# The second stream of a two-layer encoder: its loads on another queue, its multiplies behind another instruction, a third buffer

## The chip, the cores and the metric

The kernel runs on one core of one Trainium2 chip. The metric is the device time of one execution in microseconds (us); lower is better. TensorE is called PE, VectorE DVE, ScalarE ACT, GpSimd POOL and SyncE SP. A "q" behind an engine's name (SPq, ACTq) is its sequencer, which issues transfers and waits for semaphores.

## The reference, cut to what matters

Two layers over 256 positions of width 2048, batch 1, float32. Before each layer, six modulation vectors of 2048 are computed from one conditioning vector `c` by a matrix of 2048 x 12288 a layer; they shift, scale and gate the two halves of the layer.

```python
c_act = jax.nn.silu(c)
for l in range(DEPTH):                                   # DEPTH = 2
    mod = c_act @ ada_w[l] + ada_b[l]                    # [1, 6 * 2048]
    sh1, sc1, g1, sh2, sc2, g2 = split(mod, 6)
    h = rmsnorm(x, norm_mix_g[l]) * (1.0 + sc1) + sh1
    y = four_mixers(h @ w_in[l] + b_in[l])               # rglru, attention, hyena, mlstm
    x = x + g1 * (y @ w_out[l])
    h = rmsnorm(x, norm_ffn_g[l]) * (1.0 + sc2) + sh2
    x = x + g2 * ((silu(h @ w1[l]) * (h @ w3[l])) @ w2[l])
return rmsnorm(x, final_g)
```

## The kernel before, in words

Activations lie transposed (features on the 128 partitions, 256 positions on the free axis). All weights of the large products are streamed once from HBM in tiles of 128 x 1024 float32 (512 KB, called `raw`; 764 in all), in one order written out in `weight_items`.

**The weight stream.** A tile passes through four engines. SP loads it into one of six `raw` buffers (L327). ACT rounds it to `hi` (L342), DVE computes the remainder `lo = raw - hi` (L343), and PE multiplies with both (L389, L391 to L393), which gives nearly float32 precision. `hi` and `lo` have three buffers each, so a rounding waits until PE is done with the tile three places earlier. `fetch` keeps loads six tiles and the splits three tiles ahead of PE in program order; the splits have a raised priority. The first eight k-blocks of layer 0's input projection are used unsplit (L386).

**The modulation stream.** The matrix of the modulation, transposed, is 192 blocks of 128 output columns, each in two halves of 128 x 1024: 384 half columns of 512 KB. They do not go through PE. For each one `ada_load` loads a half column (tile `ada`, or `ad` from another pool for some of the first 64), and `ada` multiplies it on DVE by the broadcast activation `cb` and sums along the row (L465, with a short second instruction that reads the sum). The first 64 run ahead of layer 0; the other 320 are spread by `RATES` over the weight tiles: after the products of each tile, `ada(rate)` adds the rate to an account, and each whole unit emits one multiply. The rate is 1 a tile in layer 0's mixer and output projection, about 0.53 (8/15, then 28/53) in layer 0's feed-forward part, 24/43 in layer 1's mixer, and small after that; the last multiply comes early in layer 1's feed-forward part.

**The order.** Each engine runs its instructions strictly in order. The order is made at build time by a list scheduler with a simulated clock: an instruction is taken when its inputs are ready by that clock, earlier ones in program order first. `issue_after(ins)` adds one bound: what the block emits stands behind `ins` if it is on the same engine. So the loads of the modulation (`load`, L315) stand on SP's queue behind the latest weight load `self.last`; the multiplies stand behind one early instruction of the first norm (`self.after`) and are otherwise free. From the 59th multiply on, `ada_load` keeps two half columns loaded or under way, the one about to be multiplied included, in two buffers (`NADA` = 2).

**Transfers.** All transfers of the kernel share eight completion semaphores in turn, so that a transfer also waits until the one eight places before it has landed.

Of the kernel before, what the change touches and what calls it, by code (L numbers as in the profile page):

```python
# [11 lines left out]
F32 = mybir.dt.float32  # L12
F32R = mybir.dt.float32r
AF = mybir.ActivationFunctionType
ALU = mybir.AluOpType
# [218 lines left out]
class Lazy:  # L234


    def __init__(self, n, make):
        self.n, self.make, self.made = n, make, []
# [8 lines left out]


class Net:
    NRAW, NHL, NADA = 6, 3, 2  # L250

    BUFS = dict(h=16, y=16, p=4, s=10, e=9)
    TAGS = dict(h="h", w3="y", pl="s",
# [5 lines left out]
    def __init__(self, ctx, tc, d):  # L259
        self.tc, self.nc, self.d = tc, tc.nc, d  # L260
        self.n = 0
        self.last = self.after = None
        e = ctx.enter_context
        self.cp = e(tc.tile_pool(name="cp", bufs=1))
        self.wp = e(tc.tile_pool(name="wp", bufs=self.NHL))
        self.sp = e(tc.tile_pool(name="sp", bufs=1))
        self.tp = e(tc.tile_pool(name="tp", bufs=5))
        self.yp = e(tc.tile_pool(name="yp", bufs=12))
        self.pa = e(tc.tile_pool(name="pa", bufs=3, space=PSUM))
        self.pm = e(tc.tile_pool(name="pm", bufs=5, space=PSUM))  # L270
        nc = self.nc
        self.par = self.cp.tile([P, DEPTH, NPAR], F32, name="par")
        nc.sync.dma_start(self.par, d["par"])
        self.ident = self.cp.tile([P, P], F32, name="ident")
        nc.sync.dma_start(self.ident, d["k_ident"])
        self.misc = self.cp.tile([P, 16], F32, name="misc")
        nc.sync.dma_start(self.misc, d["k_misc"])
        self.one = self.misc[:, 0:1]
# [52 lines left out]
    def _split(self):  # L331
        k = self.n_split
        n, whole = self.items[k][1:]
        t = self.raw.pop(k)
        self.n_split += 1
        if whole:
            self.hl[k] = (t, None)
            return
        with self.tc.high_priority(offset=1500):
            hi = self.wp.tile([P, 1024], F32R, tag="hi", name=self.nm("hi"))  # L340
            lo = self.wp.tile([P, 1024], F32R, tag="lo", name=self.nm("lo"))
            self.nc.scalar.activation(hi[:, :n], t[:, :n], AF.Copy)  # L342
            self.nc.vector.tensor_tensor(lo[:, :n], t[:, :n], hi[:, :n].bitcast(F32), ALU.subtract)  # L343
        self.hl[k] = (hi, lo)

    def fetch(self):
# [91 lines left out]

    def ada_load(self):

        at = self.ada_at
        while self.ada_got < min(len(self.ada_items), at + (6 if at < 58 else self.NADA)):
            n = self.ada_got
            l, b, h = self.ada_items[n]
            if n < 64 and n % 3:
                t = self.pair("ad")
            else:
                t = self.wp.tile([P, 1024], F32, tag="ada", name=self.nm("ada"), bufs=self.NADA)
            self.load(t, self.d["ada"][l, b, :, h * 1024:(h + 1) * 1024])
            self.ada_tiles[n] = t  # L450
            self.ada_got += 1

    def ada(self, n):

        nc = self.nc
        self.ada_left += n
        while self.ada_left >= 0.999 and self.ada_at < len(self.ada_items):
            self.ada_left -= 1
            self.ada_load()
            l, b, h = self.ada_items[self.ada_at]  # L460
            t = self.ada_tiles.pop(self.ada_at)
            self.ada_at += 1
            acc, mod = self.acc[l], self.mod[l]
            with self.tc.issue_after(self.after) if self.after else nullcontext():
                nc.vector.scalar_tensor_tensor(t, t, 1.0, self.cb[:, h * 1024:(h + 1) * 1024], ALU.mult, ALU.mult,  # L465
                                               accum_out=acc[:, b, h:h + 1])
            j, k = b // 16, b % 16
            if h == 0:
                continue
            if l == 0 and j < 2:  # L470
                m = mod[:, b:b + 1]
                nc.vector.scalar_tensor_tensor(m, acc[:, b, 0:1], acc[:, b, 1:2], self.pc(l, "ada_b", b), ALU.add, ALU.add)
                if j:
                    nc.vector.scalar_tensor_tensor(self.gain[l, j][:, k:k + 1], m, 1.0, self.pc(l, "nmix", k), ALU.add, ALU.mult)
            elif k == 15:
                c = slice(j * 16, j * 16 + 16)
                nc.vector.tensor_tensor(mod[:, c], acc[:, c, 0], acc[:, c, 1], ALU.add)
                nc.vector.tensor_tensor(mod[:, c], mod[:, c], self.pc(l, "ada_b", j * 16, 16), ALU.add)
                if j in (1, 4):
                    nc.vector.scalar_tensor_tensor(self.gain[l, j], mod[:, c], 1.0, self.pc(l, "nmix" if j == 1 else "nffn", 0, 16),  # L480
                                                   ALU.add, ALU.mult)
# [775 lines left out]
```

## Time and profile before

| | |
|---|---|
| time, median of 3 runs | 2627.47 us (2624.53 to 2630.35) |
| the profiled execution: its time, its span | 2628.5 us, 2626.7 us |
| PE, DVE, ACT busy share of the span | 95%, 70%, 44% |
| mean granted TensorE clock | 0.981 of full speed |
| moved by DMA | 629.63 MB, mean 240 GB/s |
| roundings, remainders | 737 each, mean 1038 and 1210 ns |
| multiplies of the modulation | 384, mean about 1250 ns |

Read it as follows. The busy share of PE counts matmuls whose ends are modelled; where PE waits for a weight tile, this shows as idle time of its weight load (PEld) and of the matmul behind it. A wait is put down to what ended it. Idle time of the other three engines costs nothing unless PE waits for it later. By the norms' instructions in the trace, the time falls into five stages: up to 204 us the start (filters, first 64 half columns), to 621 us layer 0's mixer and output projection, to 1411 us its feed-forward part, to 1865 us layer 1's mixer and output projection, to 2616 us its feed-forward part.

### The profile page before, as it was taken

Reading aid. Unit: us, or ns where it says so; the run is one execution under the profiler, and the core shown is the slowest. Engines: PE = TensorE matmul, PEld = TensorE weight load, DVE = VectorE, ACT = ScalarE, POOL = GpSimd, SP = SyncE. Lnnn points to the kernel's source line nnn. Section 1 sums busy time; section 2 is a strip of 40 time slices with the busy share of each in tenths; the row PEclk is TensorE's granted clock in tenths of the full one; section 3 lists DMA queues with packets and bytes.
Section 4 is the critical chain, followed back from the end, with each engine's and each line's share of the span. In section 5 each row is a group of like instructions: output and inputs, shape, how many; then the busy total and the mean of one; then the engine's idle time right before and its main releaser. Section 6 shows DMA issues by size and latency. Waiting matters only on the chain. (4 is left out here: it accounts for less than half of the span.)

```text
span 2626.7 us, 38926 instructions
## 1 busy us (share of the span) xinstructions
PE 2503.5 (95%) x14962; PEld 2167.8 (83%) x14962; DVE 1827.2 (70%) x2862; ACT 1164.0 (44%) x1790; POOL 157.3 (6%) x142
## 2 busy tenths in 40 slices
PE   7989989998999999999998998999899999999998
PEld 3468878798888888778888998989888888888887
DVE  6987576688777677776788767776765555555555
ACT  4432343444444344334444445554444444434443
POOL 2101010020000000000011110002100000000001
PEclk9889999999999999999999999999899999999999
DMA  7988777688888888788887766657666665665564
GB/s 260 351 312 270 242 258 243 206 290 283 275 273 297 264 266 278 264 266 270 266 283 249 267 230 224 218 178 246 221 218 188 187 191 187 185 190 191 188 182 132
DMA packets 180719, 629.63 MB, mean 240 GB/s; under 512 B 20162, under 2 KB 20371, under 8 KB 180531
## 3 DMA queue, kind: packets, MB, share of 16 engines
q1 hardware_dynamic: 177076, 620.84, 71.5%
q10 hardware_dynamic: 3456, 6.29, 0.6%
q8 instruction: 117, 1.92, 0.3%
q14 instruction: 70, 0.57, 0.1%
HBM read 618.67 MB, written 8.39 MB: 239 GB/s over the span
## 5 line engine op out<-in xcount | busy, mean ns | idle before, releaser
L342 ACT ACTIVATE hi<-raw 128x1024 fp32r<-128x1024 f32 (+2 forms) x737 | 763.7, 1038 | 801.7 <-PE a L389 340.4
L393 PE MATMUL a<-h,lo 128*128 128x256 f32 x3848 | 1077.4, 286 | 25.8 <-DVE lo L343 25.2
L343 DVE TENSOR_TENSOR lo<-raw,hi 128x1024 fp32r<-128x1024 f32 (+2 forms) x737 | 887.5, 1210 | 281.5 <-ACT hi L342 280.8
L389 PE MATMUL a<-h,hi 128*128 128x512 f32 x2624 | 914.8, 397 | 0.0
L393 PEld LDWEIGHTS a<-h,lo 128*128 128x128 f32 x3848 | 733.4, 192 | 57.8 <-DVE lo L343 45.3
L465 DVE SCALAR_TENSOR_TENSOR ada<-ada,cb 128x1024 f32<-128x1024 f32 x342 | 425.8, 1246 | 392.8 <-DMA ada<-in_ada 392.3
L389 PEld LDWEIGHTS a<-h,hi 128*128 128x128 f32 x2624 | 485.5, 188 | 108.2
L389 PE MATMUL a<-g,hi 128*128 128x512 f32 x1352 | 463.0, 396 | 0.0
L393 PE MATMUL a<-g,lo 128*128 128x256 f32 x1408 | 370.8, 280 | 5.6 <-DVE lo L343 5.3
L391 PE MATMUL a<-h,hi 128*128 128x256 f32 x1224 | 363.0, 299 | 10.5 <-ACT h L549 6.7
L392 PE MATMUL a<-h,hi 128*128 128x256 f32 x1224 | 359.0, 294 | 6.1 <-DVE h L551 6.1
L393 PEld LDWEIGHTS a<-g,lo 128*128 128x128 f32 x1408 | 264.0, 188 | 23.7 <-DVE lo L343 12.2
L389 PEld LDWEIGHTS a<-g,hi 128*128 128x128 f32 x1352 | 243.3, 188 | 47.9
L391 PEld LDWEIGHTS a<-h,hi 128*128 128x128 f32 x1224 | 240.8, 198 | 18.2 <-ACT h L549 8.0
L392 PEld LDWEIGHTS a<-h,hi 128*128 128x128 f32 x1224 | 241.5, 197 | 12.4 <-DVE h L551 7.1
L514 POOL TENSOR_TENSOR sq<-sq,sq 128x256 f32<-128x256 f32 x65 | 71.6, 1102 | 1717.0 <-issue 1405.4
L386 PE MATMUL a<-h,raw 128*128 128x256 f32 x688 | 167.5, 395 | 3.3 <-DMA raw<-in_w_in 3.3
L386 PEld LDWEIGHTS a<-h,raw 128*128 128x128 f32 x688 | 132.7, 198 | 34.6 <-issue 12.5
L1151 DVE SCALAR_TENSOR_TENSOR x<-a,mod,x 128x256 f32<-128x256 f32 x228 | 100.3, 476 | 22.6 <-PE a L393 22.6
L1172 ACT ACTIVATE s<-s 128x256 f32<-128x256 f32 x82 | 34.3, 418 | 115.2 <-DVE s L1169 115.2
L1168 ACT ACTIVATE s<-a 128x256 f32<-128x256 f32 x82 | 31.5, 384 | 114.0 <-PE a L393 114.0
L415 ACT ACTIVATE g<-s 128x256 fp32r<-128x256 f32 x88 | 36.1, 410 | 68.2 <-DVE s L1173 62.9
(268 smaller groups left out, 2188.5 us busy)
## 6 DMA issues: line engine op xcount, KB each, us to landing
raw<-in_w SPq DMA_DIRECT2D x496, 512.0 KB, 4.7
ada<-in_ada SPq DMA_DIRECT2D x342, 512.0 KB, 6.1
raw<-in_w_in SPq DMA_DIRECT2D x168, 512.0 KB, 5.5
raw<-in_w_out SPq DMA_DIRECT2D x64, 512.0 KB, 5.7
ad<-in_ada SPq DMA_DIRECT2D x42, 512.0 KB, 7.9
raw<-in_w SPq DMA_DIRECT2D x32, 384.0 KB, 3.2
spectra<-sl ACTq DMA_DIRECT2D x24, 256.0 KB, 6.9
spec<-spectra SPq DMA_DIRECT2D x24, 256.0 KB, 6.3
```

The costliest lines, as they stand in the source:

```text
L342: self.nc.scalar.activation(hi[:, :n], t[:, :n], AF.Copy)
L343: self.nc.vector.tensor_tensor(lo[:, :n], t[:, :n], hi[:, :n].bitcast(F32), ALU.subtract)
L386: mm(o, hi[:, c], a[:, :T], start=first and b == 0, stop=last, skip_group_check=True)
L389: mm(ps[b], hi[:, c], a, start=first, stop=False, skip_group_check=True)
L391: mm(o, hi[:, c], a[:, :T], start=first and b == 0, stop=False, skip_group_check=True)
L392: mm(o, hi[:, c], a[:, T:], start=False, stop=False, skip_group_check=True)
L393: mm(o, lo[:, c], a[:, :T], start=False, stop=last, skip_group_check=True)
L415: self.nc.scalar.activation(dst[:, :T], src, AF.Copy)
L465: nc.vector.scalar_tensor_tensor(t, t, 1.0, self.cb[:, h * 1024:(h + 1) * 1024], ALU.mult, ALU.mult, accum_out=acc[:, b, h:h + 1])
L514: nc.gpsimd.tensor_tensor(self.sq, self.sq, t, ALU.add)
L1151: i = self.nc.vector.scalar_tensor_tensor(self.x[k], o, g, self.x[k], ALU.mult, ALU.add)
L1172: nc.scalar.activation(s, s, AF.Silu)
```

## The change

From the 65th half column on (`n >= 64`) the load is issued by ACT instead of SP, and stands behind the latest rounding emitted so far (`self.hi_at`), not behind the latest weight load. Each multiply also stands behind the latest remainder emitted so far (`self.lo_at`). The `ada` tile has three buffers instead of two, and two half columns are kept loaded or under way as before. The rates, the number of transfers and their sizes stay.

```diff
 class Net:
-    NRAW, NHL, NADA = 6, 3, 2
+    NRAW, NHL, NADA = 6, 3, 3
...
         self.last = self.after = None
+        self.hi_at = self.lo_at = None
...
-            self.nc.scalar.activation(hi[:, :n], t[:, :n], AF.Copy)
-            self.nc.vector.tensor_tensor(lo[:, :n], t[:, :n], hi[:, :n].bitcast(F32), ALU.subtract)
+            self.hi_at = self.nc.scalar.activation(hi[:, :n], t[:, :n], AF.Copy).ins
+            self.lo_at = self.nc.vector.tensor_tensor(lo[:, :n], t[:, :n], hi[:, :n].bitcast(F32), ALU.subtract).ins
...
     def ada_load(self):
+        nc = self.nc
         at = self.ada_at
-        while self.ada_got < min(len(self.ada_items), at + (6 if at < 58 else self.NADA)):
+        while self.ada_got < min(len(self.ada_items), at + (6 if at < 58 else self.NADA - 1)):
...
-            self.load(t, self.d["ada"][l, b, :, h * 1024:(h + 1) * 1024])
+            src = self.d["ada"][l, b, :, h * 1024:(h + 1) * 1024]
+            if n >= 64:
+                with self.tc.issue_after(self.hi_at) if self.hi_at else nullcontext():
+                    nc.scalar.dma_start(t, src)
+            else:
+                self.load(t, src)
...
-            with self.tc.issue_after(self.after) if self.after else nullcontext():
+            with (self.tc.issue_after(self.after) if self.after else nullcontext()), \
+                    (self.tc.issue_after(self.lo_at) if self.lo_at else nullcontext()):
                 nc.vector.scalar_tensor_tensor(t, t, 1.0, self.cb[:, h * 1024:(h + 1) * 1024], ALU.mult, ALU.mult,
                                                accum_out=acc[:, b, h:h + 1])
```

## Rows read from the trace of the kernel before

**Rows 1.** Windows, one for each stage: busy us by engine, granted clock, DMA share, GB/s.
```profile
204.00:621.00 417.00, 390.10 (x2466) 348.69 (x2464) 294.56 (x514) 162.35 (x296) 45.90 (x42) 0.98 0.76 256
621.00:1411.00 790.00, 763.56 (x4360) 653.58 (x4360) 587.89 (x866) 345.36 (x475) 14.31 (x14) 0.99 0.82 272
1411.00:1865.00 454.00, 433.50 (x3198) 406.75 (x3198) 331.87 (x543) 230.81 (x382) 49.94 (x43) 0.97 0.68 227
1865.00:2616.00 751.00, 745.40 (x4360) 654.82 (x4360) 444.77 (x590) 342.14 (x472) 12.41 (x14) 0.99 0.60 186
```
**Rows 2.** Waits of PEld, stages two to five: us in total, times, longest us.
```profile
PEld a L393 <- DVE lo L343: 5.8, 6, 2.0
...
PEld a L393 <- DVE lo L343: 45.7, 63, 3.3
...
PEld a L393 <- DVE lo L343: 7.5, 6, 3.8
...
PEld a L393 <- DVE lo L343: 0.5, 1, 0.5
```
**Rows 3.** Waits of DVE for the modulation's loads, stages two, three and four.
```profile
DVE ada L465 <- DMA ada<-in_ada: 100.3, 65, 3.8
...
DVE ada L465 <- DMA ada<-in_ada: 189.2, 105, 4.4
...
DVE ada L465 <- DMA ada<-in_ada: 89.7, 46, 6.0
```
**Rows 4.** DVE, timeline around one such wait in stage three.
```profile
913.58 1.22 DVE L343 TENSOR_TENSOR lo<-raw,hi 128x1024 fp32r<-128x1024 f32 x1
919.04 1.23 DVE L465 SCALAR_TENSOR_TENSOR ada<-ada,cb 128x1024 f32<-128x1024 f32 x1 [4.23 <-DMA ada<-in_ada]
...
920.52 1.22 DVE L343 TENSOR_TENSOR lo<-raw,hi 128x1024 fp32r<-128x1024 f32 x1
```
**Rows 5.** PE, the same timeline.
```profile
920.05 0.63 PE L389 MATMUL a<-h,hi 128*128 128x512 f32 x2
921.79 0.51 PE L393 MATMUL a<-h,lo 128*128 128x256 f32 x2 [1.11 <-DVE lo L343]
```
**Rows 6.** SP's queue, the same timeline.
```profile
909.13 1.85 SPq L327 DMA_DIRECT2D raw<-in_w  x2
911.03 0.42 SPq L315 DMA_DIRECT2D ada<-in_ada  x1
```
**Rows 7.** The tile ada: multiplies of stages two, three, four; landing in stage three.
```profile
L465 DVE SCALAR_TENSOR_TENSOR ada<-ada,cb x97: 1210/1225/2295, 204.1 to 619.7; 128x1024 f32<-128x1024 f32 x97
...
L465 DVE SCALAR_TENSOR_TENSOR ada<-ada,cb x144: 1208/1225/1384, 623.9 to 1393.7; 128x1024 f32<-128x1024 f32 x144
DMA to landing us min/median/max: 4.2/6.3/8.4
...
L465 DVE SCALAR_TENSOR_TENSOR ada<-ada,cb x65: 1210/1225/1753, 1413.4 to 1847.9; 128x1024 f32<-128x1024 f32 x65
```
**Rows 8.** ACT, timeline in stage five, after the last multiply.
```profile
2120.74 1.06 ACT L342 ACTIVATE hi<-raw 128x1024 fp32r<-128x1024 f32 x1 [1.93 <-PE a L389]
2123.56 1.06 ACT L342 ACTIVATE hi<-raw 128x1024 fp32r<-128x1024 f32 x1 [1.76 <-PE a L389]
```
**Rows 9.** DVE, the same stretch.
```profile
2121.84 1.23 DVE L343 TENSOR_TENSOR lo<-raw,hi 128x1024 fp32r<-128x1024 f32 x1 [2.03 <-ACT hi L342]
2124.65 1.22 DVE L343 TENSOR_TENSOR lo<-raw,hi 128x1024 fp32r<-128x1024 f32 x1 [1.59 <-ACT hi L342]
```
**Rows 10.** The tile spectra: ACT's only transfers, all in the first stage.
```profile
L684 ACTq DMA_DIRECT2D spectra<-sl x24: 326/334/975, 80.1 to 161.7; - x24
...
DMA to landing us min/median/max: 5.3/6.7/8.7
```
**Rows 11.** Waits of ACT in stage two.
```profile
ACT L846 <- DVE v L842: 18.4, 1, 18.4
```
**Rows 12.** Windows of 65.7 us: the slice with the highest DMA rate.
```profile
65.70:131.40 65.70, 59.58 (x170) 31.46 (x168) 59.37 (x123) 29.21 (x58) 11.80 (x6) 0.90 0.93 351
```

## The prediction, made before the changed kernel was run

> **What bounds the kernel now.** I read the windows by stage first. Stages three and five are the feed-forward parts of the two layers and do the same work on PE: 4360 matmuls each. Stage three takes 790 us and stage five 751 us, a difference of 39 us [rows 1]. What differs is the modulation: 144 multiplies lie in stage three [rows 7], and stage five holds only its last few. So 39 us is about what the second stream costs layer 0's feed-forward part, and it is the largest thing that a change to this stream alone can win there. In stage five PE is busy 745 of 751 us, so the tensor work itself is the floor.
>
> Next, the waits of PE's weight loads, stage by stage. In stage three they wait 63 times, 45.7 us in all, for a remainder from DVE; in stage five 0.5 us in all; in the two mixers 5.8 and 7.5 us [rows 2]. DVE is busy only 588 of 790 us in stage three [rows 1], so it is late and not overloaded. The waits of DVE say why: 105 of the 144 multiplies wait for their load, 189 us in all, 1.8 us each on average [rows 3].
>
> The timeline shows one case from cause to effect. SP issues two weight loads and, behind them, a load of the modulation at 911.03 [rows 6]. DVE finishes a remainder at 914.80, then comes to the multiply, whose half column is there only at 919.04, 8.0 us after its issue: 4.23 us idle. The next remainder starts at 920.52 [rows 4], and PE, out of split tiles, idles 1.11 us before the matmul that needs it [rows 5]. The roundings and remainders hold only three tiles, so DVE standing still for that long empties them.
>
> The landing in stage three takes 4.2 to 8.4 us, median 6.3 [rows 7]. As the mean wait is 1.8 us over the stalled ones, the built order puts a multiply some 4.5 to 5 us behind the issue of its load, earlier than the load can be there. That, not the rate of the transfers, is the fault: stage three moves 272 GB/s [rows 1], and the first part of the kernel reached 351 [rows 12].
>
> **The change, part by part.** *The distance from load to multiply.* After the change a load stands behind the latest rounding, and its multiply, emitted one unit of the account later, behind the remainder that is the latest by then. In stage three a unit comes every 1.9 tiles, so two tiles lie between in about 8 of 9 cases and one in the others. I take the tile's rhythm from stage five, where nothing disturbs it: roundings start 2.82 us apart (2120.74, 2123.56) and last 1.06 [rows 8]; a remainder starts 1.10 behind its rounding and lasts 1.23 [rows 9]. The load goes out 1.06 us after the start of its rounding. With two tiles between, the multiply can start at 2 x 2.82 + 1.10 + 1.23 = 7.97 on the same scale, 6.9 us behind the issue; with one tile, 4.1 us. Against the median landing of 6.3 that is no wait in most two-tile cases (I estimate 0.3 us on average from the spread up to 8.4), and about 2.2 us in the one-tile cases. Sum over 144: 128 x 0.3 + 16 x 2.2 = 74 us of DVE waiting in place of 189.
>
> *What that is worth on PE.* A remainder ends 2.33 us after its buffer comes free and is needed two tiles later, at 5.64: 3.3 us to spare. A multiply takes 1.2 of them [rows 7], so about 2 us of waiting is still hidden. Only the one-tile cases reach past that, by some tenths; with the activations' work that DVE also does between, I leave 6 us of the 39. Bounds: nothing gained here (the landing moves with the issue), and 39 us gained. I take 33, near the upper end, because the stalls of [rows 3] are the one difference between stages three and five.
>
> *The load's issue on ACT.* ACT's only transfers now took 334 ns each to issue, at most 975, and the sequencer does nothing else meanwhile [rows 10]. 320 loads make 107 us. In stage three that is 144 x 0.33 = 48 us more on an engine busy 345 of 790 [rows 1], just behind a rounding, with the next rounding free to start only when PE gives up a buffer: ACT sat idle 1.76 us for that [rows 8]. Hidden there. In the mixers, 97 + 65 loads [rows 7] make 54 us on an engine busy 162 of 417 and 231 of 454 us; a chain that runs through ACT (softmax, gates) can meet some of it. Between 0 and 54 us; I take 2 us, near zero, because of the idle time. If a load had to wait for its buffer on ACT, every rounding behind it would wait too. The third buffer excludes this: the load that is emitted just before multiply m needs the buffer of multiply m - 2, a unit or more old.
>
> *SP's queue.* It loses 320 loads, and weight loads no longer stand behind one. In stages three and five roundings wait for PE and not for weights, so nothing is won there. Some waits for a weight tile in the mixers may go; I count nothing.
>
> *The mixers.* DVE's waits for loads there, 100 and 90 us [rows 3], shrink in the same way, less in stage two, where a unit comes every tile and the distance is 4.1 us. PE's waits for remainders there are 5.8 + 7.5 = 13.3 us [rows 2], the most that can be won by this way; I take 4 us. The first 64 half columns keep their queue; the third buffer for a third of them I count at nothing, for lack of any wait of PE on them in these rows.
>
> The Trainium skill, "DMA: Bandwidth & Descriptors", section "Issuing engines are not separate DMA queues", says that transfers issued from different engines run on the same 16 DMA engines and that a second issuing engine saves only the sequencer's issue time. The trace can't test this for these loads, as all stand on SP's queue. By that rule alone the landing stays at its 6.3 us, which is what the sum above uses; the sum holds only through the distance, and if the rule were wrong and loads landed near their fastest 4.2 us, even one-tile cases would be nearly free and the gain would be 39 + 4.
>
> **The sum.** 33 (stage three) + 4 (mixers) - 2 (issue on ACT) = 35 us. The profiled execution took 2628.5 us, 1.0 above the median; 2628.5 - 35 = 2593.5, and against the median 2592.5. I say **2593 us**.
>
> **Rivals.**
> *The multiply still comes too early.* If the schedule's clock lets the load go out on ACT later than behind its rounding (ACT's queue is in order, and in stage two it stood 18.4 us for one DVE result [rows 11]), or lets only one tile lie between, the waits stay near 2 us and move rather than go. For it: the order is built with a clock that took landing for 4.5 to 5 us. Against it: the two new bounds hold in any order. A load that is late by one tile in all of stage three returns to 4.1 us of distance and 2.2 us of waiting, more than the 1.8 of now: the 33 us are lost, and with the mixers' small sums the time is 2622 to 2633. This is also where the skill's rule leads if the distance did not grow. Chance 0.12.
>
> *Half of it.* The distance grows, but DVE, with the multiplies now bunched behind remainders, misses the spare 3.3 us more often. Half of the 33 is kept: 2606 to 2622. Chance 0.10.
>
> *Slower: the issue delays what stands behind it on ACT in the mixers.* There a rounding shares ACT with the softmax, the gates and the evacuation of PSUM, and PE waits on results of these chains. If each of the 162 loads put its 334 ns into such a chain, that costs 54 us; with 33 won in stage three the time is 2628.5 - 33 + 54 = 2649. The point from which it decides: more than 38 us, so 0.24 us for each of the 162, or an issue that takes up to the 975 ns of [rows 10] and holds roundings in stage three as well. Against it: ACT is idle half of the mixers, and only one instruction in many there is one that PE waits for. Chance 0.13, 2634 to 2665.
>
> **How the numbers follow.** The forecast, 2580 to 2606, has 0.65. Its own range comes from the bounds: 39 + 13 gained at the most (2577), 20 at the least. Half 0.10, nothing 0.12, slower 0.13. For 8 in 10 the range takes the forecast, the half and a part of the nothing: 2581 to 2627. A measurement of this kernel tells 0.2%, 5 us, from no change: faster (below 2622) is the forecast and the half, 0.75; same 0.11; slower 0.14.
>
> **What the changed profile would show.** Right: stage three 755 to 762 us for the same 4360 matmuls; PE's weight loads waiting for remainders there under 10 us instead of 45.7; DVE's waits for the modulation's loads there below 80 us; issues of `ada` on ACT's queue of about 0.33 us, each right behind a rounding; the landing unchanged at about 6 us or shorter. Stages two and four within 5 us of 417 and 454. Wrong: stage three above 775 us, with DVE still waiting at the multiplies; or ACT's roundings waiting for the issue of a load, or for its buffer, and with them a longer stage two or four.

## The result and the profile after

The changed kernel took 2562.75 us (median of 4 runs, 2561.3 to 2564.05) against 2626.09 us for the kernel before on the same chip (median of 4 runs, 2624.53 to 2630.35). The ratio is 0.9756, 95% interval 0.9739 to 0.9773: 2.4% faster, and faster than the range that was forecast (2581 to 2627).

The page of the changed kernel, parts 1 and 3: busy time, and the transfers by queue. Below it are the same rows of the kernel before.

```profile
PE 2470.3 (96%) x14962; PEld 2164.6 (85%) x14962; DVE 1839.4 (72%) x2862; ACT 1160.4 (45%) x1788; POOL 151.6 (6%) x142
...
q1 hardware_dynamic: 130996, 453.05, 53.9%
q10 hardware_dynamic: 49536, 174.09, 19.3%
```
```profile
PE 2503.5 (95%) x14962; PEld 2167.8 (83%) x14962; DVE 1827.2 (70%) x2862; ACT 1164.0 (44%) x1790; POOL 157.3 (6%) x142
...
q1 hardware_dynamic: 177076, 620.84, 71.5%
q10 hardware_dynamic: 3456, 6.29, 0.6%
```

The matmuls are the same 14962. PE's idle time fell by 32 us (2626.7 - 2503.5 = 123 before, 2561.4 - 2470.3 = 91 after) and its busy time by 33 us. The ends of matmuls are modelled, so busy time can hold waiting too: layer 0's feed-forward stage had 764 us of it before and has 745 now, for the same work at the same granted clock of 0.99. A second queue (q10, ACT's) carries 168 MB more than before, the 320 loads of 512 KB that SP's queue carried.

Windows of the changed kernel, one for each stage, cut at the same work as [rows 1] (the first at the same number of matmuls, the others at the norms):

```profile
0.00:211.00 211.00, 169.09 (x577) 103.88 (x578) 159.68 (x332) 83.90 (x166) 31.09 (x30) 0.94 0.83 298
211.00:605.00 394.00, 385.19 (x2467) 348.52 (x2466) 292.71 (x514) 161.99 (x297) 48.51 (x42) 0.99 0.78 270
605.00:1356.00 751.00, 745.20 (x4363) 654.52 (x4362) 599.20 (x868) 345.87 (x475) 14.46 (x14) 0.99 0.85 287
1356.00:1801.00 445.00, 425.63 (x3196) 403.54 (x3196) 336.02 (x543) 226.22 (x379) 45.07 (x42) 0.98 0.70 231
1801.00:2551.00 750.00, 744.88 (x4364) 654.10 (x4362) 445.40 (x590) 342.45 (x472) 12.50 (x14) 0.99 0.60 186
```

Beside 204, 417, 790 to 791, 453 to 454 and 751 to 752 us before: layer 0's feed-forward stage wins 40 us and now takes as long as layer 1's, layer 0's mixer wins 23, layer 1's mixer 8, layer 1's feed-forward stage 1 to 2, and the first stage loses 7. PE's idle time shows this only in part. In layer 0's mixer 417 - 390 = 27 us of PE were not busy before and 394 - 385 = 9 us are now, which is 18 of the 23 us. In layer 1's mixer it hardly changed (453 - 433 = 20 us, then 445 - 426 = 19): the 8 us there came out of PE's busy time, for the same 3196 matmuls, and no row says why.

The waits of DVE for the modulation's loads after the change, in layer 0's mixer and in its feed-forward stage (before: [rows 3]), and what PE's weight loads still wait for in the feed-forward stage (before: [rows 2]):

```profile
DVE ada L474 <- DMA ada<-in_ada: 20.4, 19, 2.6
...
DVE ada L474 <- DMA ada<-in_ada: 11.7, 14, 1.9
```
```profile
PEld rb L542 <- POOL v L539: 2.0, 1, 2.0
PEld a L393 <- DVE h L560: 1.9, 1, 1.9
PEld a L392 <- ACT h L558: 1.6, 1, 1.6
PEld ss L532 <- ACT sq L521: 1.1, 1, 1.1
```

100.3 us became 20.4, and 189.2 became 11.7. The 45.7 us for which weight loads waited for remainders in the feed-forward stage have no row any more; what is left there belongs to the norm.

The timeline shows how it works now. First DVE, then ACT, in the feed-forward stage:

```profile
865.27 1.21 DVE L344 TENSOR_TENSOR lo<-raw,hi 128x1024 fp32r<-128x1024 f32 x1
866.40 1.22 DVE L474 SCALAR_TENSOR_TENSOR ada<-ada,cb 128x1024 f32<-128x1024 f32 x1
```
```profile
863.93 1.06 ACT L343 ACTIVATE hi<-raw 128x1024 fp32r<-128x1024 f32 x1 [1.02 <-PE a L390]
863.94 0.33 ACTq L455 DMA_DIRECT2D ada<-in_ada  x1
866.75 1.06 ACT L343 ACTIVATE hi<-raw 128x1024 fp32r<-128x1024 f32 x1 [1.76 <-PE a L390]
869.52 1.06 ACT L343 ACTIVATE hi<-raw 128x1024 fp32r<-128x1024 f32 x1 [1.72 <-PE a L390]
869.53 0.33 ACTq L455 DMA_DIRECT2D ada<-in_ada  x1
```

A multiply follows a remainder without a wait, and the load goes out two tiles apart from the next one. The load stands behind a rounding in the order, but is issued 0.01 us after the rounding's start and not after its end: the sequencer goes on while the engine works.

### The profile page after: what moved, and what is told of

Its sections match the earlier page's. It is cut to its first block, busy times and chain, and to the rows that moved or that the text cites. A ratio compares the mean times of both kernels' runs of the same rounds, so it can differ in the third digit from the quotient of the medians.

```text
span 2561.4 us, 38913 instructions
## 1 busy us (share of the span) xinstructions
PE 2470.3 (96%) x14962; PEld 2164.6 (85%) x14962; DVE 1839.4 (72%) x2862; ACT 1160.4 (45%) x1788; POOL 151.6 (6%) x142
## 5 line engine op out<-in xcount | busy, mean ns | idle before, releaser
L394 PEld LDWEIGHTS a<-h,lo 128*128 128x128 f32 x3848 | 735.2, 191 | 21.9 <-DVE lo L344 6.3
L1178 DVE TENSOR_TENSOR s<-s,a 128x256 f32<-128x256 f32 x82 | 34.4, 420 | 35.9 <-ACT s L1177 35.9
L558 ACT ACTIVATE h<-h,mod 128x256 fp32r<-128x256 f32 (+1 forms) x64 | 29.5, 501 | 62.8 <-DVE h L554 36.4
```

The source lines that it names most:

```text
L394: mm(o, lo[:, c], a[:, :T], start=False, stop=last, skip_group_check=True)
L1178: nc.vector.tensor_tensor(s, s, ps[0][:, :T], ALU.add)
```

## The experiments

Theory A: the cause is the time between a load's issue and its multiply, so that DVE no longer stands still. Theory B: the cause is the queue, that is, weight loads and modulation loads out of each other's way. Theory C: the cause is the third buffer. The change has three parts (the queue, the bound of the multiplies, the third buffer), and all eight combinations of them were run, the kernel before and the changed one among them; six further kernels change one size, or take away one bound or one suspected cost. All stages in the table are windows of each kernel's own trace, cut at the same work, from one execution each; "us" is the median. The ratio is to the kernel before on the chip of that run, where its median was 2626.09, 2623.82, 2628.48 or 2631.59 us, so kernels of different chips are compared by ratio.

| run | us | ratio to before (95%) | start | mixer 0 | FFN 0 | mixer 1 | FFN 1 |
|---|---|---|---|---|---|---|---|
| before | 2626.09 | 1 | 204 | 417 | 791 | 453 | 752 |
| the change | 2562.75 | 0.9756 (0.9739 to 0.9773) | 211 | 394 | 751 | 445 | 750 |
| bound of the multiplies only | 2584.26 | 0.9843 (0.9829 to 0.9858) | 204 | 419 | 751 | 447 | 750 |
| queue only | 2615.96 | 0.9971 (0.9956 to 0.9987) | 204 | 434 | 768 | 452 | 752 |
| third buffer only | 2625.48 | 1.0017 (0.9999 to 1.0035) | 210 | 411 | 785 | 453 | 752 |
| change without the bound | 2589.33 | 0.9870 (0.9853 to 0.9887) | 209 | 397 | 763 | 455 | 751 |
| change without the third buffer | 2574.80 | 0.9803 (0.9780 to 0.9825) | 202 | 413 | 750 | 445 | 751 |
| change without the queue | 2571.13 | 0.9783 (0.9763 to 0.9803) | 213 | 403 | 749 | 446 | 750 |
| loads on ACT not bound | 2571.47 | 0.9790 (0.9769 to 0.9811) | 209 | 406 | 750 | 444 | 750 |
| two buffers at first, then three | 2556.63 | 0.9729 (0.9709 to 0.9748) | 202 | 394 | 751 | 446 | 749 |
| before, multiplies on a resident tile | 2575.55 | 0.9789 (0.9773 to 0.9804) | 224 | 398 | 750 | 442 | 750 |
| the same without loads | 2574.09 | 0.9784 (0.9767 to 0.9801) | 224 | 398 | 750 | 442 | 750 |
| two, then three buffers, no loads | 2556.86 | 0.9718 (0.9702 to 0.9734) | 203 | 396 | 751 | 447 | 749 |
| two, then three buffers, three ahead | 2574.00 | 0.9786 (0.9767 to 0.9804) | 215 | 404 | 749 | 445 | 749 |

**The bound of the multiplies only.**

```diff
-    NRAW, NHL, NADA = 6, 3, 3
+    NRAW, NHL, NADA = 6, 3, 2
...
-        while self.ada_got < min(len(self.ada_items), at + (6 if at < 58 else self.NADA - 1)):
+        while self.ada_got < min(len(self.ada_items), at + (6 if at < 58 else 2)):
...
-            if n >= 64:
-                with self.tc.issue_after(self.hi_at) if self.hi_at else nullcontext():
-                    nc.scalar.dma_start(t, src)
-            else:
-                self.load(t, src)
+            self.load(t, src)
```

> Only the new bound of the multiplies (behind the latest remainder); loads on SP's queue behind the latest weight load, two buffers, as before. If the distance from a load's issue to its multiply is the cause (theory A), this alone moves most multiplies behind the landing: layer 0's feed-forward stage near 755 us of 790, DVE's waits for the modulation's loads below 100 us of 405 in all, total about 2575 to 2585. If the second queue is the cause (theory B: loads stood behind weight loads on SP's queue and landed late for that), the multiplies still wait and the total stays at 2615 to 2627. If the third buffer is the cause (theory C), the total stays at 2615 to 2627 as well.

2584 us, as theory A had it. The feed-forward stage has the whole of its gain from this one bound: 751 us, and DVE's waits there went from 189.2 us to this:

```profile
DVE lo L344 <- ACT hi L343: 116.1, 125, 1.8
...
DVE ada L470 <- DMA ada<-in_ada: 0.6, 2, 0.4
```

DVE now waits for roundings, as it does in layer 1's feed-forward stage, and these come when PE frees a buffer. Layer 1's mixer has its gain too. Layer 0's mixer has none of it: 419 us, its DVE waits still at 91.9 us in 46 waits.

**The queue only.** The loads by ACT as in the change; two buffers, and the multiplies bound by `self.after` alone.

> Only the loads from the 65th on by ACT's queue, each behind the latest rounding; two buffers, multiplies bounded as before. Theory A: the scheduler's clock still puts a multiply where it believes that the load has landed, 4.5 to 5 us behind its issue; the landing gets 0.6 us shorter, so the waits shrink by a third at most and the total is 2605 to 2625. Theory B: most of the gain, 2565 to 2580. Theory C: 2615 to 2627, and ACT's roundings may wait for a buffer.

2616 us, as theory A had it and against B. The profiled execution took 2621.7 us, 6 above the median; in it the feed-forward stage wins 23 us, but layer 0's mixer loses 17. There ACT holds roundings for a multiply, which the row of ACT's waits shows; that this makes up the 17 us was not shown:

```profile
ACT hi L343 <- DVE ada L473: 24.8, 10, 5.8
```

**The third buffer only.** `NADA` = 3 with two half columns ahead; the rest as before.

> Only the third buffer; two half columns loaded or under way, loads on SP's queue, multiplies bounded as before. Theory A: a load goes out earlier by what it waited for its buffer, and the scheduler's clock moves the multiply up with it: 2610 to 2630. Theory B: no change, 2620 to 2630, and the first stage 7 us longer as in the changed kernel if the third buffer is what lengthens it. Theory C: 2565 to 2585.

2625 us, no change that can be told: layer 0's mixer wins 6 us, its feed-forward stage 6, and the first stage loses 6. Theory C falls as the cause of the whole.

**The change without the bound of the multiplies.**

```diff
-            with (self.tc.issue_after(self.after) if self.after else nullcontext()), \
-                    (self.tc.issue_after(self.lo_at) if self.lo_at else nullcontext()):
+            with self.tc.issue_after(self.after) if self.after else nullcontext():
```

> The changed kernel without the bound of the multiplies: loads on ACT's queue behind the latest rounding, three buffers. Theory A: most of the gain is lost, because the multiply goes back to where the scheduler's clock expects the landing: 2600 to 2625, DVE waits for loads above 200 us. Theory B or C: the gain stays, 2560 to 2575.

2589 us: neither. Theory A said that most would be lost, and by the ratios a little over half was kept (1.3% of 2.4%). Layer 0's mixer has nearly all of its gain without the bound (397 us, DVE's waits 45.5 us). In the feed-forward stage the multiplies do wait again, 154.5 us of 189.2, yet PE loses much less by it than before:

```profile
DVE ada L473 <- DMA ada<-in_ada: 154.5, 102, 4.8
```
```profile
PEld a L394 <- DVE lo L344: 12.9, 12, 1.9
```

63 waits of 45.7 us have become 12 of 12.9. The other kernels without the bound line up between: 186 us of DVE's waiting with 34 us lost in this stage (third buffer only), 152 with 17 (queue only). So the loss doesn't grow in proportion to DVE's waits. Why 155 us cost 12 here and 189 cost 39 before was not settled; the multiplies stand at other places between the remainders in this order.

**The change without the third buffer.** `NADA` = 2, with the queue and both bounds.

> The changed kernel with two buffers instead of three, two half columns loaded or under way as before. The load emitted before multiply m now needs the buffer of multiply m - 1. Theory A: that multiply is one unit old, so in layer 0's feed-forward stage nothing is lost (750 to 755 us); in layer 0's mixer, with a unit every tile, ACT waits for the multiply with roundings behind it: total 2560 to 2580. Theory C: 2610 or more. If the third buffer is what costs 7 us in the first stage, the first stage gets those back.

2575 us, as theory A had it, with the place that it named: all of the loss is in layer 0's mixer, 413 us, where a unit comes every tile. The rows of ACT's and of DVE's waits there:

```profile
ACT hi L343 <- DVE ada L474: 43.0, 12, 12.9
```
```profile
DVE ada L474 <- DMA ada<-in_ada: 66.0, 46, 6.5
```

The load waits on ACT for the multiply that frees its buffer, roundings wait behind it, and the load then goes out too late for its own multiply. The first stage is back at 202 us.

**The change without the queue.** All loads by `self.load` on SP's queue; three buffers and the bound of the multiplies.

> The changed kernel with all loads on SP's queue behind the latest weight load, three buffers, multiplies behind the latest remainder. Theory A: nearly all of the gain stays, 2562 to 2580. Theory B: most of it is lost, 2600 to 2627.

2571 us, as theory A had it; B falls. What the queue adds on top is 9 us in layer 0's mixer (403 against 394). DVE waits 71.8 us there and SP's loads wait 29.1 us for a multiply to free a buffer, with weight loads behind them.

**The loads on ACT without their bound.** `nc.scalar.dma_start(t, src)` without `issue_after(self.hi_at)`.

> The changed kernel without the bound of the loads: ACT issues them wherever the scheduler puts them. The third buffer lets a load go out as soon as its buffer is free, earlier than behind the latest rounding. Theory A: the distance only grows: 2558 to 2566. A rival: early loads meet more of the weight loads, or hold ACT, 2570 or more.

2571 us, the rival. DVE waits hardly more than in the change (21.5 us in layer 0's mixer against 20.4), but that stage takes 406 us. ACT meets three long waits there, put down to a transfer of the modulation; in the change no wait of ACT of that kind is longer than 3.6 us in the whole run:

```profile
ACT hi L343 <- DMA ada<-in_ada: 10.2, 1, 10.2
...
ACT vt L739 <- DMA ada<-in_ada: 7.9, 1, 7.9
ACT ht L982 <- DMA ada<-in_ada: 7.6, 1, 7.6
```

The bound of the loads is worth these 12 us in that stage; that these three waits make up all of it was not shown.

**Two buffers for the first 64 half columns, three from then on.**

```diff
-                t = self.wp.tile([P, 1024], F32, tag="ada", name=self.nm("ada"), bufs=self.NADA)
+                late = n >= 64 and n % 3 == 2
+                t = self.wp.tile([P, 1024], F32, tag="adb" if late else "ada", name=self.nm("ada"), bufs=1 if late else 2)
```

> The changed kernel with two buffers for the first 64 half columns and three from then on (the third from a pool of its own, the same memory). If the third buffer is what made the first stage 7 us longer, through another order there, the total is 2553 to 2558 and the first stage is as before; if the longer first stage comes from the loads on ACT or from the order elsewhere, the total stays at 2561 to 2565.

2557 us, as expected, and the fastest of all kernels here, though its interval overlaps that of the change. The first stage takes 202 us instead of 211; the other four are the same within 1 us. So the third buffer costs up to 9 us where it wasn't needed. Windows of 15 us, the change first, then this kernel, with the granted clock third from the end:

```profile
175.00:190.00 15.00, 8.23 (x43) 7.63 (x44) 10.59 (x23) 1.01 (x2) 0.00 (x0) 0.79 0.87 337
190.00:205.00 15.00, 14.18 (x76) 13.28 (x76) 9.45 (x19) 8.57 (x16) 0.00 (x0) 0.75 0.47 150
```
```profile
175.00:190.00 15.00, 11.60 (x69) 10.47 (x68) 11.30 (x21) 6.43 (x12) 0.00 (x0) 0.89 0.91 342
190.00:205.00 15.00, 15.00 (x100) 14.07 (x99) 14.86 (x28) 6.90 (x13) 3.72 (x4) 1.00 0.95 341
```

In the change the last of layer 0's normalised blocks comes from ACT at 192 us instead of 182, and ACT waits 16.5 us there for the modulation's results instead of 7.8, which in that order come later; PE idles and then runs at a granted clock of 0.75, which is a part of the time at the lower of its two levels, 1.2 and 2.4 GHz.

**The kernel before, its later multiplies on a resident tile.** The loads are kept, and nothing reads them; the kernel leaves the later modulation out of its output.

```diff
+        self.junk = self.cp.tile([P, 1024], F32, name="junk")
+        nc.vector.memset(self.junk, 0.0)
...
-                nc.vector.scalar_tensor_tensor(t, t, 1.0, self.cb[:, h * 1024:(h + 1) * 1024], ALU.mult, ALU.mult,
+                u = t if self.ada_at <= 64 else self.junk
+                nc.vector.scalar_tensor_tensor(u, u, 1.0, self.cb[:, h * 1024:(h + 1) * 1024], ALU.mult, ALU.mult,
                                                accum_out=acc[:, b, h:h + 1])
```

> The kernel before, with the 320 later multiplies reading and writing one resident tile of zeros; all loads stay on SP's queue with their two buffers and nothing reads them, so that layer 0's later modulation is its bias alone and the output differs. If DVE's waits at the multiplies are the whole cause, in the mixers too (theory A), the stages are those of the changed kernel: layer 0's mixer 390 to 400 us, its feed-forward stage 747 to 752, total 2552 to 2566. If loads on SP's queue, in the way of the weight loads, cost something of their own (theory B), layer 0's mixer stays at 405 us or more and the total above 2570.

2576 us, 10 above theory A's range, and all of that lies in the first stage (224 us): with nothing to wait for, the scheduler put 42 of the later multiplies into it (3 before), where DVE is then busy 204 of 224 us. The other stages are as theory A had them: 398, 750, 442 and 750 us with all loads on SP's queue and moved as before. In the feed-forward stage and in layer 1's mixer the multiplies are as many as before, so their gain goes with DVE's waits. Layer 0's mixer is not so clean: it holds 59 multiplies here and 97 before. For it the kernel with two, then three buffers and no later loads counts (below): 96 multiplies, none of which waits for a load, and 396 us. PE's waits in layer 0's mixer, before and in this run:

```profile
PE m L884 <- DVE lf L882: 8.5, 1, 8.5
PE m L813 <- DVE aq L811: 3.9, 2, 2.3
PE a L393 <- DVE lo L343: 3.7, 4, 1.8
...
PE m L857 <- DVE pe L851: 1.6, 1, 1.6
PE m L1053 <- DVE hn L761: 1.4, 1, 1.4
```
```profile
PE m L887 <- DVE lf L885: 5.9, 1, 5.9
PE rb L536 <- POOL v L533: 2.0, 1, 2.0
PE ss L526 <- ACT sq L515: 1.0, 1, 1.0
```

In this mixer the remainder was only one of several DVE results that PE waited for: the gates of the mLSTM (`lf`), the rotated queries (`aq`), the softmax (`pe`), the convolution (`hn`).

**The same without the loads.**

```diff
+            if n >= 64:
+                self.ada_tiles[n] = None
+                self.ada_got += 1
+                continue
```

> The same without the 320 later loads: the multiplies work on the resident tile, nothing is moved for them (the modulation is left out as above). Theory A: as the run with the loads kept, within 8 us. Theory B: faster than that run by more than 8 us.

2574 us, every stage within 1 us of the run with the loads, while layer 0's mixer moves 141 GB/s instead of 270. With nothing waiting for it, the traffic costs nothing that can be told. Nor does its place on SP's queue: with the loads kept, they wait 59.6 us in that mixer for a load before them to land, with weight loads behind, and without them the stage is no shorter.

**Two, then three buffers, no later loads.** The two edits above on the kernel of 2557 us.

> The changed kernel with two buffers for the first 64 half columns, its 320 later loads left out and their multiplies on the resident tile (the modulation is left out as above): what the loads still cost after the change. Theory A: 2548 to 2557, nearly nothing left. Theory B, or a cost of the issue on ACT: 2530 to 2545.

2557 us: the same as with the loads. In this kernel nothing is left of the second stream's transfers in the time. Against the bound alone (419 us in layer 0's mixer, DVE's waits 91.9), the later loads are all that is gone, with the multiplies on the resident tile, and the stage takes 396 us; since the traffic cost nothing in the run before, this points to the waits for the loads.

**Three half columns ahead in the three buffers.** `at + 3` instead of `at + 2`, on the kernel of 2557 us.

> The changed kernel with two buffers for the first 64 half columns and, from then on, three half columns loaded or under way in the three buffers instead of two. The distance grows by one unit, but a load needs the buffer of the multiply just before it. If what is left in layer 0's mixer is waiting for landings: 2545 to 2553. If the free buffer is what matters there (ACT then waits for the multiply, with roundings behind it): layer 0's mixer at 405 us or more, total 2565 or more.

2574 us, near the second branch: layer 0's mixer 404 us, and the first stage 215 besides, which wasn't expected. DVE's waits for loads there, 23.9 us, are no shorter than with two ahead (21.9 us), so more distance wins nothing. Roundings wait for a multiply only 13.7 us there, no more than in the change (15.6), so the explanation that I gave does not hold; why this order is slower stays open.

## Why the prediction was wrong, and where it was right

*The mechanism held.* Late landings made DVE stand still, and PE ran out of split tiles in layer 0's feed-forward stage. The bound alone moves that stage to 751 us, and the resident tile, with the loads still made, to 750.

*The step that failed is "The mixers".* It took PE's waits for remainders, 13.3 us, as the most that could be won there, and took 4. The gain was 23 + 8 = 31 us. The bound was read from one kind of wait. In layer 0's mixer PE also waited for other DVE results: its waits for DVE sum to 20.3 us before (remainders 3.7 of them) and 5.2 after, and the wait for the gates `lf` alone fell from 8.5 to 4.9. The stage's time goes with PE's waits for all engines: 8.9 us with 394, 14.7 with 406 (loads not bound), 23.2 with 413 (no third buffer), 26.4 with 417 (before), 34.4 with 434 (queue only). With DVE's waits for loads it doesn't go as closely: 45.5 us go with 397 (no bound) and 21.5 with 406. In layer 1's mixer the size was wrong as well, but by which of PE's waits it came stays open. The run on the resident tile has 442 us there, and DVE's waits for loads there are 89.7 us before, 0.7 in the change and 74.6 without the bound, where the stage takes 455. So the gain goes with DVE's waits, yet PE's idle time did not fall.

*The third buffer was weighed as a safeguard only.* The text says that it excludes a wait on ACT, and gives no price for its absence. In layer 0's mixer it carries most of the gain, with the other two parts in place: 413 us without it, 394 with it. It doesn't exclude the wait. Loads still wait on ACT for a multiply. By the rows of ACT's waits, roundings wait 15.6 us for multiplies (43.0 without the buffer), and one step of the gates stands behind such a load for 5.26 us. The lines are DVE's, ACT's and PE's:

```profile
375.15 1.21 DVE L474 SCALAR_TENSOR_TENSOR ada<-ada,cb 128x1024 f32<-128x1024 f32 x1
```
```profile
376.40 0.34 ACTq L455 DMA_DIRECT2D ada<-in_ada  x1
376.78 0.42 ACT L888 ACTIVATE ga<-gates 128x256 f32<-128x256 f32 x1 [5.26 <-DVE ada L474]
```
```profile
381.16 1.11 PE L893 MATMUL m<-lf,ident 64*64 64x256 f32 x2 [4.91 <-DVE lf L891]
```

`lf` is computed from `ga`, so PE's longest wait left in that mixer lies at the end of this chain. Little of it is owed to the load: without later loads PE still waits 3.9 us there.

*The first 64 half columns at nothing.* Wrong: the third buffer cost 7 us there by another order, and 9 against the kernel that avoids it.

*Stage three, 33 of 39 us.* A term somewhat too small: 40 us. The load goes out at the start of the rounding and not at its end, so the distance is 1.06 us longer than worked out; the median landing is 5.7 us against 6.3; DVE's waits are 11.7 us and not 74. "Below 10 us" for PE's waits for remainders was right: there is no row of them.

*The issue on ACT, 2 us of 0 to 54.* Not measured by itself. Issues of 0.33 us run while ACT computes, and the mixers became shorter, so the slower rival did not come; its way, work on ACT behind a load, is there in the lines above, with little effect.

*Together.* Forecast 33 + 4 - 2 = 35. Measured between the two profiled executions: 2628.5 - 2563.2 = 65 us; by stages 40 + 31 + 2 - 7 = 66, with the rounding of the windows.

*The rivals.* "The multiply still comes too early" is what happens without the bound: 155 us of waits stay. But it doesn't give the time that the text worked out, since PE loses less by these waits in that order. The rule of the Trainium skill, "DMA: Bandwidth & Descriptors", section "Issuing engines are not separate DMA queues", that a second issuing engine saves only issue time, agrees with the traces: in stage three the median landing is 6.3, 5.8, 6.1 and 6.6 us from SP's queue (before, bound only, change without the queue, third buffer only) and 6.0, 6.4, 6.0 and 5.7 us from ACT's (queue only, change without the bound, without the third buffer, the change). By itself the queue gave 8 us. Where the queue paid, in layer 0's mixer, the likely reason is that a load that waits for its buffer no longer stands ahead of weight loads; that was not tried by itself, and in the run on the resident tile such waits on SP's queue cost nothing that can be told.

## What to carry to other kernels

When an in-order engine stands still for a late input, don't price the gain by the bottleneck's waits for the one result that heads the list: everything behind the stall is late. The sum of its waits for all results of the stage is nearer (26.4 us in layer 0's mixer, where 23 were won). Even that can fall short, as busy time can hold waiting; a stage that does the same work undisturbed is the better measure (39 us by it, 40 won). A scheduler that places a consumer where its clock believes the transfer has landed can be corrected by an order bound to work that paces the kernel, and then one buffer more than are in flight makes the issue itself wait less. Give that buffer only to the phase that needs it: a free buffer elsewhere changes the order, and here it cost up to 9 us.

## What the runs showed of the hardware that was not expected

A transfer that follows an activation in ACT's program is issued while the activation runs, 0.01 us after its start (863.94 against 863.93), in 0.334 us as a median over 320. Of the 302 rows of such issues in the timeline, 172 start within 0.02 us of the start of a rounding. In the stretch shown, the next rounding starts 2.82 us after one with an issue behind it (863.93 to 866.75) and 2.77 us after one without (866.75 to 869.52), so no cost of such an issue can be told there. When the load waits for a multiply to free its buffer, the roundings behind it wait as well (43.0 us in the run without the third buffer, 15.6 us in the change, both in layer 0's mixer).
